# Pair products in another order, values split in place, evictions ahead of splits: a two-layer hybrid encoder block on one core

## The chip, the cores and the metric

The kernel runs on one NeuronCore of a Trainium2 chip. The metric is the time of one execution on the device in microseconds (us); the median of several runs is compared.

## The reference

Two layers on 512 frames of width 1024, in float32. Each layer normalises x, multiplies it with one wide matrix and feeds two recurrent branches, then a feed-forward part and a gated embedding:

```python
h = rmsnorm(x, norm1_g[i]);  z = h @ w_in[i] + b_in[i]
# branch A: mLSTM, 4 heads, dk = dv = 256 (q, k through a causal convolution and swish)
y_m = sigmoid(mo) * head_layernorm(mlstm(mq, mk, mv, mi, mf), m_norm_g[i])
# branch B: retention, 4 heads, dk = 256, dv = 512, rotary on q and k, decay per head
y_r = silu(rg) * head_layernorm(retention(rope(rq), rope(rk), rv), r_norm_g[i])
x = x + (sigmoid(gm) * (y_m @ w_bm[i]) + sigmoid(gr) * (y_r @ w_br[i])) @ w_out[i]
h2 = rmsnorm(x, norm2_g[i])
x = x + square(relu(h2 @ w_ff1[i] + b_ff1[i])) @ w_ff2[i] + b_ff2[i]
h3 = rmsnorm(x, norm3_g[i])
x = x + sigmoid(h3 @ w_pe_gate[i]) * (p[i] @ w_pe[i])
# after both layers: rmsnorm(x, final_g)
```

## The kernel before, in words

**Matmuls.** Every operand is split into a high part, rounded to the PE's format, and a low part, the rest; a product is three matmuls: high x high, high x low, low x high. All weights stream from HBM as *units*, in the order of `unit_list`. A `T8` unit is 128 output columns of a 1024-row matrix (24 matmuls of 512 columns). A `V` unit serves values, `PE` the embedding. A `PAIR` unit is 256 output columns in a scheme with seven products instead of eight (P1 to P7, each 12 matmuls of 256 columns): queries and keys of the retention, some gates, and the second feed-forward matrix. A `WIDE` unit is the same for the retention's values.

**Pieces of a pair.** P1 and P5 use piece A, P6 and P2 piece B, P3 and P7 piece C, P4 piece D. A, B and C are loaded into *raw* buffers of 128x1024 float32 (`fill_raws`, on SP's queue, four buffers plus one more in the first part of a layer); `prep_next` splits them: ACT writes the high part `wh`, DVE the low part `wl` (line 287). DVE makes the second half of B from A and C (line 421) and D from both halves of B (line 424). Sums of weight blocks that the loads read (`t1`, `t3`, `t2`) are made in HBM by accumulating DMAs on POOL's queue (`step`, line 331), paced along the matmuls. Split pieces have three buffers, D has one. `in_order` keeps loads, and splits on ACT and on DVE, in the order of the program. The order before is A, C, B, D.

**Banks.** Within a pair the products share PSUM banks: P1, P6, P7, P4 accumulate in one (a), P5 and P3 in another (c), P2 has a third (b). After each product the sum so far is read out (`done`, the *eviction*): in `pair_tiles` by ACT or DVE, in `ff2` by DVE adds into x (lines 1398, 1400). So P6 waits for the eviction of P1, P3 for that of P5, P7 for that of P6, P4 for that of P7. `run_pair` issues P1, P5, then `flush()`, then P6, P2, P3, P7; P4 is put into `later` and run by the next `flush()`, which is in the next pair, after four k steps of a `T8` tile, in the first block of an attention, before a head's scores, or after the first transposed tile of the gating.

**Order of instructions.** The program is written with a framework that gives each instruction a priority by its place in the program. A planner then fixes the order on each engine ahead of the run: with estimated durations, each engine takes the ready instruction that stands earliest in the program. On the chip every engine runs its list in that order.

**Retention.** For heads 0 and 2 a `WIDE` unit makes the values of two heads; those of the second are written to HBM (`rv_spill`) and read back by `rv_load` on POOL's queue into four of the six temporary tiles, then split into the value tiles. `r_gates` makes two gate tiles of a head by a pair, `r_out` the other two, transposes the four normalised output tiles (`back`) and multiplies and splits each.

**Norms.** A norm has one tile for its sum of squares and one for the factor of each frame, shared by all norms. The feed-forward part runs in four blocks `b`, each a group of `T8` pairs (`ff1`) and four `PAIR` units (`ff2`, o00 to o33); the embedding's two units stand before the last four pairs, and `flush()` after them.

Names in the trace: `l0r2o1a` is layer 0, retention, head 2, second gate pair, bank a; `l0r1brq`, `l0r1brk` are the query and key pairs of head 1; `l0o12` is the feed-forward pair of block 1, columns 2; `wh_A` is the high part of a piece A.

Of the kernel before, what the change touches and what calls it, by code (L numbers as in the profile page):

```python
# [42 lines left out]
P = 128  # L43
# [10 lines left out]
LOOK = 2  # L54
WARM = 11
# [36 lines left out]
PIECE = {"A": ("B11", "t1"), "C": ("B22", "t3"), "B": ("B21",), "D": ()}  # L92
# [22 lines left out]
READY = {"P1": 2, "P4": 2, "P5": 3, "P2": 4, "P6": 4, "P3": 4, "P7": 5}  # L115
# [35 lines left out]
def unit_list(i):  # L151
# [77 lines left out]
    u.append(("PE", 0))  # L229
    u.append(("PE", 1))  # L230
    pairs(ff_order()[1])
# [4 lines left out]
def build(ctx, tc, ins, out):  # L236
# [114 lines left out]
    loads = [(n, x) for n, x in order if x != "D" and x not in (("t4", 0), ("t4", 1))]  # L351
# [4 lines left out]
    cur["room"], cur["more"] = (), None  # L356
# [5 lines left out]
    def fill_raws(most=RAWS + 1):  # L362
        while at["load"] < len(loads) and len(raws) + len(kept) < most:
            n, x = loads[at["load"]]
            r = None
            if n in cur["room"] and cur["more"] not in raws:
                cur["more"] = n, x
                r = cur["low"].tile([P, UN], F32, name=f"wr{at['load']}", tag="wrx", bufs=1)
            elif len(raws) - (cur["more"] in raws) >= RAWS:
                break  # L370
            raws[n, x] = r = r or wpool.tile([P, UN], F32, name=f"wr{at['load']}", tag="wr", bufs=RAWS)
# [18 lines left out]
    def prep_next():  # L390
# [3 lines left out]

        w = Q if x == "D" else UN
# [8 lines left out]
        if r is None:  # L404
            r = raws.pop((n, x))
        if gates:
# [10 lines left out]
        if x == "A" or wide and x[0] == "t2":  # L417
            kept[n, x] = r
        elif x == "C":

            ve.tensor_tensor(raws[n, "B"][:, Q:], kept.pop((n, "A"))[:, Q:], r[:, :Q], OP.add)  # L421
        elif x == "B":

            ve.tensor_tensor(r[:, :Q], r[:, :Q], r[:, Q:], OP.add)  # L424
            formed[n, "D"] = r
        elif wide and x[0] == "B21":
            t = cur["br"].tile([P, UN], F32, name=f"t4{n}_{x[1]}", tag=("ph", "pl")[x[1]])
            ve.tensor_tensor(t, kept.pop((n, ("t2", x[1]))), r, OP.add)
            formed[n, ("t4", x[1])] = t

# [41 lines left out]
    def run_pair(name, act, done):  # L472
# [68 lines left out]
    def pair_tiles(name, act, consume, y=None):  # L541

        y = y or [tmp(f"{name}y{d}") for d in range(2)]
        a, b = slice(0, S), slice(S, T)

        def done(x, o):
            if x == "P1":
# [11 lines left out]
            else:  # L559
                ac.activation(y[0][:, a], o, AF.Copy)  # L560
                consume(y)

        run_pair(name, act, done)
# [38 lines left out]
    class Norm:  # L602


        def __init__(self, name, i, gain, act=None, j0=0, j1=NT):
# [20 lines left out]
        def square(self, k, x, add=None):  # L626
            w = self.n * P
            x = x[:, self.s]
            if self.sum is None:
                pl = cur["last"] if self.half else opool  # L630
                sq = pl.tile([P, w if self.half else T], F32, name=f"{self.name}sum", tag="ssum", bufs=1)[:, :w]
# [58 lines left out]
        def spread(self):  # L690
# [11 lines left out]
            pl = cur["last"] if self.half else opool  # L702
            self.b = pl.tile([P, w if self.half else T], F32, name=f"{n}rb", tag="rb", bufs=1)[:, :w]
# [51 lines left out]
    def scores(nm, qh, ql, kh, kl, decay):  # L755

        flush()
# [18 lines left out]
    def attend(nm, pt, vh, vl, c0, n, num):  # L776
        ph, pl, offs = pt
        for j in range(NT):
# [5 lines left out]
            if j == 0:  # L784
# [116 lines left out]
    cur["room"] = range(room)  # L901
# [17 lines left out]
    for i in range(L):  # L919
        act_side, ph_side = ("right", "left") if i == 0 else ("left", "right")  # L920
        xa = n1.act
        if i:
            cur["low"] = phase(f"low{i}", ph_side)
            cur["tmp"], cur["ntmp"] = cur["low"], NTMP
            cur["room"] = range(i * NU // L, i * NU // L + room)
# [165 lines left out]
        def r_gates(h, w, gs):  # L1091
# [6 lines left out]
            pair_tiles(f"l{i}r{h}o{w}", xs, consume)  # L1098

        def r_out(h, num, y, gs=None):  # L1100
# [91 lines left out]
        def rv_load(h):  # L1192

            v = value_tiles(f"l{i}r{h}")
            for j in range(NT):
                t = tmp(f"l{i}r{h}vr{j}")
                gp.dma_start(t, rv_dram[i, h // 2, j])
                split(t, v[0][j][:, :T], v[1][j][:, :T])
            return v

# [102 lines left out]
        vv = rv_load(3)  # L1303
        pt = r_scores(3, qk)
        yr = acts(cur["br"], f"l{i}yr1")
# [85 lines left out]
        def ff2(b, p):  # L1391
            started = set()

            def add(q, o, op):
                y = x[2 * p + q // 2][:, (q % 2) * S:(q % 2 + 1) * S]
                if b == 0 and q not in started:
                    started.add(q)
                    ve.scalar_tensor_tensor(y, y, bcol(i, "bf2", 2 * p + q // 2), o, OP.add, op)
                else:
                    ve.tensor_tensor(y, y, o, op)  # L1400

            def done(x_, o):
# [13 lines left out]
                if b == 3 and p and x_ in ("P6", "P7"):  # L1416
# [22 lines left out]
        n3 = Norm(f"l{i}n3", i, "g3", acts(n3_pool, f"l{i}n3"))  # L1439
# [3 lines left out]
        for u in range(2):  # L1443
            _, wh, wl = unit("PE")
            for c in range(4):
# [18 lines left out]
        nn = ([Norm(f"l{i}n4{a}", i, "gf", None, 2 * a, 2 * a + 2) for a in range(2)] if last  # L1464
# [205 lines left out]
```

## Time and profile before

| | |
|---|---|
| Runs | 2347.84, 2348.01, 2348.44 us; median 2348.01 |
| Profiled execution | 2347.49 us, span from first to last instruction 2345.8 us |
| PE busy | 2320.2 us (99%), 13660 matmuls |
| DVE, ACT, POOL busy | 1722.9 us (73%), 1218.9 us (52%), 245.7 us (10%) |
| Granted TensorE clock | 0.997 on the mean |
| HBM | 212 GB/s over the span |

Busy time counts a matmul from its start to its modelled end, and matmuls overlap; a wait of PE is read from the starts of its matmuls. L442 to L444 are the matmuls of a `T8` unit, L491 to L493 those of a pair, L534 to L536 those of a wide unit.

### The profile page before, as it was taken

The numbers are of one execution on the slowest core, as the hardware profiler recorded it, in microseconds if no ns is written. First come the engines' busy times: TensorE is split into PE (matmuls) and PEld (weight loads), VectorE is DVE, ScalarE is ACT, GpSimd is POOL, SyncE is SP. The second block draws the span as 40 slices with busy tenths as digits, with TensorE's granted clock in tenths as the row PEclk, the third lists the DMA queues.
The fourth block names the chain that finished last, engine by engine and source line by source line (L and its number), as shares of the span: only waits on it lengthen the run. The fifth ranks groups of instructions, "written<-read, shape, count | busy, mean of one in ns | idle before, by whom it ended". The sixth has DMA issues, their size and how long they took to land. (4 is left out here: it accounts for less than half of the span.)

```text
span 2345.8 us, 35261 instructions
## 1 busy us (share of the span) xinstructions
PE 2320.2 (99%) x13660; PEld 2056.2 (88%) x13660; DVE 1722.9 (73%) x2658; ACT 1218.9 (52%) x1768; POOL 245.7 (10%) x369
## 2 busy tenths in 40 slices
PE   9999999999999999999999999999999999999998
PEld 7888899898898898899888888998989988998997
DVE  7878767895675577677878787778958656776785
ACT  6656444553554445446557564454536445445454
POOL 3111101100102100000321110000000020000012
PEclk9999999999999999999999999999999999999999
DMA  5666676667578667676775645434343542433431
GB/s 201 187 180 172 218 229 170 205 189 202 168 230 269 195 198 189 199 219 181 206 221 169 182 124 186 136 126 158 108 158 104 166 153 96 130 108 98 132 117 59
DMA packets 146631, 394.89 MB, mean 168 GB/s; under 512 B 15376, under 2 KB 18832, under 8 KB 146464
## 3 DMA queue, kind: packets, MB, share of 16 engines
q1 hardware_dynamic: 99952, 247.77, 32.0%
q0 software_dynamic: 31104, 117.45, 20.4%
q10 hardware_dynamic: 15408, 27.43, 3.3%
q8 instruction: 107, 1.75, 0.3%
q14 instruction: 60, 0.49, 0.1%
HBM read 373.71 MB, written 123.73 MB: 212 GB/s over the span
## 5 line engine op out<-in xcount | busy, mean ns | idle before, releaser
L286 ACT ACTIVATE wh<-wr 128x1024 fp32r<-128x1024 f32 (+1 forms) x223 | 232.2, 1044 | 276.5 <-issue 69.6
L287 DVE TENSOR_TENSOR wl<-wr,wh 128x1024 fp32r<-128x1024 f32 (+1 forms) x221 | 271.9, 1232 | 77.7 <-ACT wh L286 77.5
L286 ACT ACTIVATE wh_B<-wr 128x1024 fp32r<-128x1024 f32 x100 | 105.9, 1059 | 159.2 <-PE l0f L443 8.5
L287 DVE TENSOR_TENSOR wl_B<-wr,wh_B 128x1024 fp32r<-128x1024 f32 x100 | 121.9, 1219 | 32.5 <-ACT wh_B L286 32.3
L286 ACT ACTIVATE wh_D<-wr 128x512 fp32r<-128x512 f32 x76 | 48.0, 632 | 124.9 <-DVE wr L424 65.4
L286 ACT ACTIVATE wh_C<-wr 128x1024 fp32r<-128x1024 f32 x76 | 80.2, 1056 | 61.3 <-issue 9.2
L286 ACT ACTIVATE wh_A<-wr 128x1024 fp32r<-128x1024 f32 x76 | 79.9, 1052 | 54.7 <-PE l1f L443 9.0
L287 DVE TENSOR_TENSOR wl_C<-wr,wh_C 128x1024 fp32r<-128x1024 f32 x76 | 94.3, 1240 | 18.7 <-ACT wh_C L286 18.5
L287 DVE TENSOR_TENSOR wl_A<-wr,wh_A 128x1024 fp32r<-128x1024 f32 x76 | 92.7, 1220 | 17.3 <-ACT wh_A L286 17.3
L442 PE MATMUL l1f<-l1n2h,wh 128*128 128x512 f32 x256 | 99.8, 390 | 0.0
L442 PE MATMUL l0f<-l0n2h,wh 128*128 128x512 f32 x256 | 99.8, 390 | 0.0
L444 PE MATMUL l0f<-l0n2h,wl 128*128 128x512 f32 x256 | 99.7, 389 | 0.0
L444 PE MATMUL l1f<-l1n2h,wl 128*128 128x512 f32 x256 | 99.7, 389 | 0.0
L443 PE MATMUL l1f<-l1n2l,wh 128*128 128x512 f32 x256 | 99.6, 389 | 0.0
L443 PE MATMUL l0f<-l0n2l,wh 128*128 128x512 f32 x256 | 99.6, 389 | 0.0
L287 DVE TENSOR_TENSOR wl_D<-wr,wh_D 128x512 fp32r<-128x512 f32 x76 | 52.4, 689 | 33.2 <-ACT wh_D L286 31.7
L421 DVE TENSOR_TENSOR wr<-wr,wr 128x512 f32<-128x512 f32 x76 | 52.1, 686 | 14.6 <-DMA wr<-wpairs 13.1
L444 PEld LDWEIGHTS l0f<-l0n2h,wl 128*128 128x128 f32 x256 | 48.0, 188 | 10.2
L444 PEld LDWEIGHTS l1f<-l1n2h,wl 128*128 128x128 f32 x256 | 48.1, 188 | 10.1
L443 PEld LDWEIGHTS l1f<-l1n2l,wh 128*128 128x128 f32 x256 | 48.1, 188 | 9.8
L442 PEld LDWEIGHTS l0f<-l0n2h,wh 128*128 128x128 f32 x256 | 48.1, 188 | 9.8
L442 PEld LDWEIGHTS l1f<-l1n2h,wh 128*128 128x128 f32 x256 | 48.1, 188 | 9.7
(5625 smaller groups left out, 8357.9 us busy)
## 6 DMA issues: line engine op xcount, KB each, us to landing
wr<-wstream SPq DMA_DIRECT2D x219, 512.0 KB, 4.2
wr<-wpairs SPq DMA_DIRECT2D x228, 256.0 KB, 2.8
wr<-wwide SPq DMA_DIRECT2D x24, 512.0 KB, 4.0
s0t<-wwide POOLq DMA_DIRECT2D x5, 1024.0 KB, 7.8
s4t<-wwide POOLq DMA_DIRECT2D x5, 1024.0 KB, 9.0
s12t<-wwide POOLq DMA_DIRECT2D x5, 1024.0 KB, 8.1
s16t<-wwide POOLq DMA_DIRECT2D x5, 1024.0 KB, 8.5
s1t<-wpairs POOLq DMA_DIRECT2D x4, 1024.0 KB, 6.7
```

The source lines that it names most:

```text
L286: a = ac.activation(hi_ap, src, AF.Copy)
L287: return a, ve.tensor_sub(lo_ap, src, hi_ap.bitcast(F32))
L421: ve.tensor_tensor(raws[n, "B"][:, Q:], kept.pop((n, "A"))[:, Q:], r[:, :Q], OP.add)
L442: te.matmul(o, sh, mh, start=first, stop=False)
L443: te.matmul(o, sh, ml, start=False, stop=False)
L444: cur["mm"] = te.matmul(o, sl, mh, start=False, stop=last)
```

## The change

- The products of a pair run as P1, P5, P2, P6, then `flush()`, then P3, P7; with `early` the flush stays after P5. Splits go A, B, C, D; loads still A, C, B, and the half of B that needs A and C is made just before B's split. P3 asks for one piece more ahead.
- Evictions of a pair, in `pair_tiles` and `ff2`, are given the priority of 250 instructions earlier.
- `rv_load` is parted: `rv_fetch` reads the values straight into the low value tile, right after the attention of the head before; `rv_split` splits them in place after the scores.
- `scores` has no `flush()`; the attention of heads 1 to 3 flushes after its second block.
- In `r_out`, two gate tiles are transposed and multiplied after P3 of the second gate pair, the other two are transposed after the pair and multiplied with the next `flush()`, behind P4.
- The norm's two tiles become one of 128x1024, handed from norm to norm, and between the first `WIDE` unit and `w_out` it serves as one more raw buffer.
- The second embedding unit moves behind the last four pairs, with a `flush()` after its third tile.

```diff
+AHEAD = 250
-PIECE = {"A": ("B11", "t1"), "C": ("B22", "t3"), "B": ("B21",), "D": ()}
+PIECE = {"A": ("B11", "t1"), "B": ("B21",), "C": ("B22", "t3"), "D": ()}
-READY = {"P1": 2, "P4": 2, "P5": 3, "P2": 4, "P6": 4, "P3": 4, "P7": 5}
+READY = {"P1": 2, "P4": 2, "P5": 3, "P2": 4, "P6": 4, "P3": 5, "P7": 5}
...
     u.append(("PE", 0))
+    pairs(ff_order()[1])
     u.append(("PE", 1))
-    pairs(ff_order()[1])
...
+    swap = {"B": "C", "C": "B"}
+    loads = [(n, swap.get(x, x)) for n, x in order if x != "D" and x not in (("t4", 0), ("t4", 1))]
+    wide0 = unit_list(0).index(("WIDE", (0, "rv0"), 0))
+    where = {n + i * NU // L: ("low", "one") if n >= wide0 else ("low",) for i in range(L) for n in range(room)}
+    free, taken = ["low", "one"] + list(range(RAWS)), {}
+    def norm_tile():
+        return opool.tile([P, 2 * T], F32, name="nr", tag="nr", bufs=1)
+    def raw_tile(a):
+        if a == "one":
+            return norm_tile()
+        pl, tag = (cur["low"], "wrx") if a == "low" else (wpool, f"wr{a}")
+        return pl.tile([P, UN], F32, name=f"wr{at['load']}", tag=tag, bufs=1)
...
+            fits = where.get(n, ()) if n * L // NU == cur["layer"] else ()
+            a = next((a for a in free if a in range(RAWS) or a in fits), None)
+            if a is None:
                 break
+            free.remove(a)
+            taken[n, x] = a
+            raws[n, x] = r = raw_tile(a)
...
+        if x == "B":
+            ve.tensor_tensor(r[:, Q:], kept.pop((n, "A"))[:, Q:], raws[n, "C"][:, :Q], OP.add)
+            give((n, "A"))
...
-        elif x == "C":
-            ve.tensor_tensor(raws[n, "B"][:, Q:], kept.pop((n, "A"))[:, Q:], r[:, :Q], OP.add)
+        elif x == "D":
+            give((n, "B"))
...
-    def run_pair(name, act, done):
+    def run_pair(name, act, done, early=False, mid=None):
...
-        product("P1")
-        product("P5")
-        flush()
-        for x in ("P6", "P2", "P3", "P7"):
+        for x in ("P1", "P5", "P2", "P6", "P3", "P7"):
             product(x)
+            if x == ("P5" if early else "P6"):
+                flush()
+            if x == "P3" and mid:
+                mid()
         later.append(last)
...
+    def ahead():
+        return tc.high_priority(AHEAD)
...
         def done(x, o):
+            with ahead():
+                evict(x, o)
+            if x == "P4":
+                consume(y)
...
     def scores(nm, qh, ql, kh, kl, decay):
-        flush()
...
-            if j == 0:
+            if j == turn:
                 flush()
...
-            attend(nm, pt, vv[0], vv[1], 0, 512, num)
+            attend(nm, pt, vv[0], vv[1], 0, 512, num, int(h > 0))
...
-            r_gates(h, 1, gs)
-            for v in range(4):
-                o = back(nm, num, v)
-                if v == 0:
-                    flush()
+            def gate(v, o):
                 ve.scalar_tensor_tensor(gs[v], o, bcol(i, "grn", 4 * h + v), gs[v], OP.mult, OP.mult)
                 split(gs[v], y[0][(4 * h) % 8 + v], y[1][(4 * h) % 8 + v])
+            def turn(a):
+                return [(v, back(nm, num, v)) for v in (a, a + 1)]
+            r_gates(h, 1, gs, mid=lambda: [gate(*t) for t in turn(0)])
+            o = turn(2)
+            later.insert(0, lambda: [gate(*t) for t in o])
...
-        def rv_load(h):
+        def rv_fetch(h):
             v = value_tiles(f"l{i}r{h}")
             for j in range(NT):
-                t = tmp(f"l{i}r{h}vr{j}")
-                gp.dma_start(t, rv_dram[i, h // 2, j])
-                split(t, v[0][j][:, :T], v[1][j][:, :T])
+                gp.dma_start(v[1][j][:, :T].bitcast(F32), rv_dram[i, h // 2, j])
             return v
+        def rv_split(v):
+            for hi, lo in zip(*v):
+                split(lo[:, :T].bitcast(F32), hi[:, :T], lo[:, :T])
...
         num = r_attend(0, pt, vv)
+        vv = rv_fetch(1)
         gs = {}
         r_gates(0, 0, gs)
-        vv = rv_load(1)
         pt = r_scores(1, qk)
+        rv_split(vv)
...
-        r_gates(1, 0, gs)
+        r_gates(1, 0, gs, early=True)
...
         num = r_attend(2, pt, vv)
+        vv = rv_fetch(3)
         qk = r_qk(3)
...
-        vv = rv_load(3)
         pt = r_scores(3, qk)
+        rv_split(vv)
...
+                with ahead():
+                    if b == 0 and q not in started:
+                        started.add(q)
+                        ve.scalar_tensor_tensor(y, y, bcol(i, "bf2", 2 * p + q // 2), o, OP.add, op)
+                    else:
+                        ve.tensor_tensor(y, y, o, op)
...
-                if b == 3 and p and x_ in ("P6", "P7"):
+                if b == 3 and p and x_ in ("P3", "P7"):
                     tile3(2 * p - 2 + (x_ == "P7"))
...
+                if c == 2:
+                    flush()
+        embed(0)
         for _, b, p in rest:
             ff2(b, p)
-        flush()
+        embed(1)
```

More of the change, by code (lines that the diff above doesn't have):

```diff
@@ L355, in build, with fill_raws @@
     room = unit_list(0).index(("T8", "w_out", 0, 0))
-    cur["room"], cur["more"] = (), None
+    wide0 = unit_list(0).index(("WIDE", (0, "rv0"), 0))
[8 more added lines that the diff above has]
+        return pl.tile([P, UN], F32, name=f"wr{at['load']}", tag=tag, bufs=1)
     def halves(n):
         return [slice(0, Q), slice(Q, UN)] if n == 1 else [slice(0, UN)]
-    def fill_raws(most=RAWS + 1):
-        while at["load"] < len(loads) and len(raws) + len(kept) < most:
+    def fill_raws(most=None):
+        while at["load"] < len(loads) and at["load"] != most:
             n, x = loads[at["load"]]
[L365 to L369, printed above, removed]
+            fits = where.get(n, ()) if n * L // NU == cur["layer"] else ()
+            a = next((a for a in free if a in range(RAWS) or a in fits), None)
+            if a is None:
                 break
-            raws[n, x] = r = r or wpool.tile([P, UN], F32, name=f"wr{at['load']}", tag="wr", bufs=RAWS)
+            free.remove(a)
+            taken[n, x] = a
+            raws[n, x] = r = raw_tile(a)
             if x:
@@ L629, in square @@
             if self.sum is None:
-                pl = cur["last"] if self.half else opool
-                sq = pl.tile([P, w if self.half else T], F32, name=f"{self.name}sum", tag="ssum", bufs=1)[:, :w]
+                if self.half:
+                    sq = cur["last"].tile([P, w], F32, name=f"{self.name}sum", tag="ssum", bufs=1)
+                else:
+                    self.own = self.own or norm_tile()
+                    sq = self.own[:, 0:w]
             else:
@@ L701, in spread @@
             te.matmul(o[:, :w], ones_r, dl, start=False, stop=True)
-            pl = cur["last"] if self.half else opool
-            self.b = pl.tile([P, w if self.half else T], F32, name=f"{n}rb", tag="rb", bufs=1)[:, :w]
+            self.b = self.own[:, T:T + w]
             ac.activation(self.b, o[:, :w], AF.Copy)
@@ L900, in build @@
     cur["tmp"], cur["ntmp"] = cur["low"], NTMP
-    cur["room"] = range(room)
+    cur["layer"] = 0
     n1 = Norm("l0n1", 0, "g1", acts(xa_pool, "l0n1"))
@@ L924, in build @@
             cur["tmp"], cur["ntmp"] = cur["low"], NTMP
-            cur["room"] = range(i * NU // L, i * NU // L + room)
+            cur["layer"] = i
         cur["br"] = phase(f"br{i}", ph_side)
```

37 lines of the change are left out of this document (19 added, 18 removed).

## The prediction

> **What bounds the kernel now.** I read the page first, for the shares of the engines.
>
> ```profile
> span 2345.8 us, 35261 instructions
> PE 2320.2 (99%) x13660; PEld 2056.2 (88%) x13660; DVE 1722.9 (73%) x2658; ACT 1218.9 (52%) x1768; POOL 245.7 (10%) x369
> ```
>
> TensorE (PE) is never idle for long: 2345.8 - 2320.2 = 25.6 us in all. The change adds and removes no matmul, so it can only move waits of PE. The waits of PE by releaser, longest first, show which ones there are (total, times, longest):
>
> ```profile
> PE l0r2o1a L491 <- ACT wh_A L286: 3.4, 1, 3.4
> PE l1o33a L491 <- DVE l1x L1400: 1.6, 1, 1.6
> PE l0o33a L491 <- DVE l0x L1400: 1.3, 1, 1.3
> PE l0m0vp L747 <- DVE wl L287: 1.3, 1, 1.3
> PE l0r0o0a L491 <- DVE l0r0o0y L558: 1.2, 1, 1.2
> PE l1r0o0a L491 <- DVE l1r0o0y L558: 1.2, 1, 1.2
> PE warm L905 <- POOL ones_r L275: 1.1, 1, 1.1
> PE l0r1brqa L491 <- DVE l0r1brqy L558: 1.0, 1, 1.0
> ...
> PE l0o12a L491 <- DVE l0x L1400: 0.7, 1, 0.7
> ```
>
> Seven of these rows are on line 491, in the pair units, 10.4 us together. The rest of the idle time (start, mLSTM part, end) lies where the diff does nothing.
>
> Idle time understates a wait here. The timeline of PE, and the granted clock by stretches, say by how much (start, duration; then stretch, PE, PEld, DVE, ACT, POOL, PEclk, DMA):
>
> ```profile
> 608.73 0.41 PE L491 MATMUL l0r2o0c<-l0xsh,wh_C 128*128 128x256 f32 x1
> 608.94 0.41 PE L492 MATMUL l0r2o0c<-l0xsl,wh_C 128*128 128x256 f32 x1
> 609.44 0.28 PE L492 MATMUL l0r2o0c<-l0xsl,wh_C 128*128 128x256 f32 x1
> 609.56 0.28 PE L493 MATMUL l0r2o0c<-l0xsh,wl_C 128*128 128x256 f32 x1
> 603.70:609.30 5.60, 5.16 (x22) 4.87 (x23) 4.06 (x10) 2.79 (x8) 0.00 (x0) 0.51 0.35 115
> ```
>
> At full clock a matmul of a pair starts 0.12 us after the one before but counts as busy for 0.28, so 0.28 - 0.12 = 0.16 us of each wait is not seen as idle. After the one wait of 3.4 us the granted clock is 0.51 for 5.6 us, and matmuls start every 0.21 us: 0.09 us lost on each of the 24 that ran there, 2.2 us more. [...]
>
> **The change part by part.** *Values in place, fetched early (worth 5.8 us).* Why did ACT hold the weight piece back by 3.4 us? ACT's timeline, the tiles' landing times (layer 0, then layer 1) and POOL's timeline:
>
> ```profile
> 598.58 0.63 ACT L286 ACTIVATE l0r3vh<-l0r3vr 128x512 fp32r<-128x512 f32 x1 [2.83 <-DMA l0r3vr<-rv_spill]
> 602.69 1.04 ACT L286 ACTIVATE wh_A<-wr 128x1024 fp32r<-128x1024 f32 x1
> DMA to landing us min/median/max: 4.4/11.1/12.1
> DMA to landing us min/median/max: 2.8/3.0/3.0
> 587.23 0.90 POOL L331 DMA_DIRECT2D s8t<-wpairs  x1 [9.98 <-DMA br_spill<-l0brs]
> 587.88 1.95 POOL L1197 DMA_DIRECT2D l0r3vr<-rv_spill  x3
> ```
>
> The reload of head 3's values is issued at 587.88, right behind a step of the weight sums, and lands after 11.1 us (3.0 in layer 1, where none is ahead). ACT takes its instructions in order, so wh_A stands behind that split. The new `rv_fetch(3)` stands before `r_qk(3)` and the eight `w_br` tiles, with all of their matmuls between it and its split, and needs none of the six temporary tiles. On POOL it waits for PE's last read of the value tile; behind it are only the next weight sums. Wait 3.4 + 0.16 + 2.2 of half clock = 5.8 us gone. At head 1 it is earlier by a pair and removes no wait.
>
> *Embedding unit behind the last pairs (3.2 us).* The two o33a rows are the last product P4 of the last feed-forward pair, waiting for the add that empties P7. Now three embedding tiles, 18 matmuls of 512 columns, stand between P7 and P4: with twice the columns of a pair's matmul some 0.24 us each, an estimate, over 4 us. 1.6 + 1.3 + 2 x 0.16 = 3.2 us. The two normalised tiles that follow P4 keep one embedding tile and six k steps of the gate product as cover; without it they would cost PE up to the 1.6 us of now.
>
> *No flush before the scores; flush after P6 (2.6 us of 3.9).* In r0o0a and r1brqa PE waits in P4 for P7's add. Two products or a few score matmuls lie between now, four products afterwards. r1brqa gives 1.0 + 0.16 = 1.2. For the two r0o0a rows, 2 x (1.2 + 0.16) = 2.7, DVE has little room:
>
> ```profile
> 403.00:430.00 27.00, 25.78 (x209) 25.30 (x208) 24.78 (x46) 19.61 (x32) 4.70 (x7) 1.00 0.62 203
> ```
>
> DVE is busy 24.78 of 27.00 us there, so some of the wait may come back at the next piece of weights. I take half, 1.4. The gating in two turns does the same instructions, with two transposed tiles more held in PSUM; I cost it at nothing, because the next head's attention or a pair covers it. If that cover fails it is a wait like r0o0a's, 1.4 us a layer.
>
> *Eviction priority, B before C, raw buffers (0.9 + 4.7 us).* o12a, an eviction behind a split, gives 0.7 + 0.16 = 0.9. Besides, going through the starts of PE's matmuls, I count 71 places in the pairs that are late by less than 0.3 us. The first and the last:
>
> ```profile
> 330.04 0.28 PE L493 MATMUL l0bgm2c<-l0xsh,wl_A 128*128 128x256 f32 x1
> 330.32 0.39 PE L491 MATMUL l0bgm2a<-l0xsh,wh_B 128*128 128x256 f32 x1
> 2285.34 0.39 PE L491 MATMUL l1o33a<-l1hh,wh_D 128*128 128x256 f32 x1 [1.58 <-DVE l1x L1400]
> 2285.56 0.28 PE L492 MATMUL l1o33a<-l1hl,wh_D 128*128 128x256 f32 x1
> ```
>
> They are late by 0.28 - 0.12 = 0.16 and 0.22 - 0.12 = 0.10; at 0.10 each, 7.1 us. Many are pieces B, which were prepared third and used second, or followers of a large wait. I take two thirds, 4.7 us; bounds 0 and 7.1.
>
> *What it costs.* The planner keeps the pieces in order, and there is one buffer for D, so D of a pair is split only after P4 of the pair before, and the next A only after D. In a feed-forward pair of now:
>
> ```profile
> 1023.41 0.28 PE L491 MATMUL l0o22a<-l0hh,wh_A 128*128 128x256 f32 x1
> 1023.65 0.28 PE L493 MATMUL l0o22a<-l0hh,wl_A 128*128 128x256 f32 x1
> 1026.24 0.28 PE L491 MATMUL l0o21a<-l0hh,wh_D 128*128 128x256 f32 x1
> 1027.65 0.28 PE L491 MATMUL l0o22a<-l0hh,wh_B 128*128 128x256 f32 x1
> 1027.83 0.63 ACT L286 ACTIVATE wh_D<-wr 128x512 fp32r<-128x512 f32 x1 [2.31 <-PE l0o21a L493]
> 1028.36 1.05 ACT L286 ACTIVATE wh_A<-wr 128x1024 fp32r<-128x1024 f32 x1
> 1028.56 0.41 DVE L1400 TENSOR_TENSOR l0x<-l0x,l0o21a 128x256 f32<-128x256 f32 x1
> 1029.83 1.21 DVE L287 TENSOR_TENSOR wl_A<-wr,wh_A 128x1024 fp32r<-128x1024 f32 x1
> ```
>
> A product takes 1027.65 - 1026.24 = 1.41 us. From the end of P4 (1027.65) until A is whole (1029.83 + 1.21 = 1031.04) it takes 3.39 us. Now four products follow P4; afterwards two, P3 and P7, and A's low part is first read by the third matmul, 1023.65 - 1023.41 = 0.24 later: 2 x 1.41 + 0.24 = 3.06 us. It is short by 0.33. The planner can put the first two matmuls of P5 ahead, which leaves 0.33 - 0.24 = 0.09. Such transitions: pairs whose predecessor's P4 is still behind, 12 in the feed-forward part and 5 in the retention part of a layer, 34 in all. 34 x 0.09 = 3.1 us; bounds 0 and 34 x 0.33 = 11.2. Second, where no P4 is behind (16 pairs a layer), only P3 lies between P6 and P7, which need the same bank: 1.41 us for 0.28 of the matmul, the 0.41 of the add and at worst a split of 1.21 in its way, 1.90. P1 and P6 stand so now, and the waits show hardly any; I take one such loss, 0.5 us, bounds 0 and 4 (eight). The shared norm tile and the extra raw buffer I cost at nothing: loads start earlier, and where the tile serves as a buffer its norm has been used up.
>
> **Sum.** 5.8 + 3.2 + 2.6 + 0.9 + 4.7 = 17.2 gained, 3.1 + 0.5 = 3.6 paid: 13.6 us off the profiled execution's 2347.49 us (span 2345.8 and 1.7 around it). The median of the runs is 2348.0, so 2334.4. All gained and nothing paid is 20.9, 2327; half gained and 4 paid is 2348.0 - 8.6 + 4 = 2343.4.
>
> **The rivals.** *A: weights become the wait (slower).* If the chain from P4 to A stretches, every one of the 34 transitions stalls. It decides at 17.2 / 34 = 0.51 us each. The row at 1028.56 shows how: with priority one more add of 0.41 can go ahead of wl_A, 0.33 + 0.41 = 0.74, and 34 x 0.74 = 25 us: 2356. Against it: the chain above already holds one add, and evictions are split between ACT and DVE in the retention part. Chance 0.08.
>
> *B: loads land too late.* B is now loaded last, behind C, into the buffer of the last C.
>
> ```profile
> 1013.82 0.88 POOL L331 DMA_DIRECT2D s16t<-wwide  x1 [8.14 <-PE l0o20a L493]
> 1015.54 0.33 SPq L379 DMA_DIRECT2D wr<-wpairs  x1
> 1024.46 1.06 ACT L286 ACTIVATE wh_B<-wr 128x1024 fp32r<-128x1024 f32 x1 [2.68 <-DMA wr<-wpairs]
> ```
>
> Beside a weight sum (1013.82) a load took 1024.46 - 1015.54 = 8.9 us until its split began. The next B can be loaded when C's split is over (1.05 + 1.21, some 2.4 us into a pair), so its split would begin at 11.3. P2 of the next pair comes at 9 x 1.41 = 12.7, and two splits must be over by then: 12.7 - 1.05 - 1.21 = 10.4. That is 0.9 us late; in each of the 12 pairs of layer 0's feed-forward part that follow a pair it makes 10.8 us, and 2348.0 - 17.2 + 3.6 + 10.8 is 2345. [...] Against B: sums run beside only some loads, and the retention part gets a buffer more. Chance 0.08.
>
> *C: the change does less than it says.* The order on every engine is fixed ahead by a planner from estimates, and priority only chooses among what it thinks ready. If the evictions stay where they are, only the early fetch and the embedding unit count: 5.8 + 3.2 - 3.6 = 5.4, 2342.6. Chance 0.10.
>
> **How the numbers follow.** Forecast 2334.4 with chance 0.74, its own range 2327 to 2343.4 from the two ends of the sum, and one us below for waits elsewhere that earlier loads may shorten. With B and C 2326 to 2346, which leaves out A and edges. About 0.2% (4.7 us) is what a measurement can tell from no change. Faster by more: the forecast, most of C and a little of B, 0.83. Within: the rest of both, 0.09. Slower: A, 0.08.
>
> **What would show it.** Right: no l0r2o1a wait on ACT, clock 1.0 throughout the retention part, no o33a and r0o0a rows, PE's idle time near 16 us. Wrong: rows of PE waiting for wl_A or wh_A at nearly every second pair of a block (A), for wh_B behind DMA in layer 0 (B), or the same r0o0a and r1brqa rows again (C).

## The result, and the profile after

Forecast: 2334.4 us. Measured: 2359.11 us median (2358.42 to 2359.59), against 2347.93 for the kernel before: ratio 1.0045, 95% interval 1.0031 to 1.0059. The change makes the kernel slower by 11.2 us. The profiled execution took 2358.42 us, its span is 2356.7, 10.9 above the span of before. The first rows of the page:

```profile
span 2356.7 us, 35318 instructions
PE 2327.9 (99%) x13660; PEld 2057.3 (87%) x13660; DVE 1719.4 (73%) x2658; ACT 1212.0 (51%) x1768; POOL 250.4 (11%) x369
```

The matmuls are as many as before, and idle time is 2356.7 - 2327.9 = 28.8 us instead of 25.6; the prediction's sign of being right was 16. The waits of PE by releaser (total, times, longest) show that the rows named in the prediction are gone, and what came for them:

```profile
PE l1r2s L463 <- ACT l1r2kh L287: 1.7, 1, 1.7
PE l0r2s L463 <- ACT l0r2kh L287: 1.7, 1, 1.7
PE l1r3brqa L512 <- ACT l1r3brqy L580: 1.6, 1, 1.6
...
PE l0r3brqa L512 <- ACT l0r3brqy L580: 0.8, 1, 0.8
PE l0r0o1a L514 <- DVE wl_A L288: 0.8, 1, 0.8
PE l1r0o1a L514 <- DVE wl_A L288: 0.8, 1, 0.8
PE l0o33c L514 <- DVE wl_C L288: 0.8, 1, 0.8
PE l0o12b L514 <- DVE wl_B L288: 0.8, 1, 0.8
PE l0o22b L514 <- DVE wl_B L288: 0.8, 1, 0.8
```

Rows of idle time understate (1.75 us before the first matmul of l0r2s, which starts 1.91 us late), so I compare starts: the *lateness* of a group of matmuls is the sum, over its starts, of the distance to the start before less that of full clock (0.118 us for a pair's 256 columns, 0.227 for 512, the commonest distances in the traces of both kernels). It can be below zero, because in some stretches matmuls of 256 columns start every 0.114 us. Summed over all groups it rose by 10.95 us, which is the change of the span. By groups, layer 0 and layer 1:

| group | before | after | change |
|---|---|---|---|
| r2o0 + r2o1 (wait for wh_A) | 7.10, 1.52 | 0.31, 0.31 | -6.8, -1.2 |
| r0o0 and r1brq (wait for P7's add) | 2.87, 1.59 | 0.94, 1.63 | -1.9, 0 |
| o33 | 1.66, 1.72 | 1.19, 0.54 | -0.5, -1.2 |
| r3brq | 0.07, 0.06 | 2.50, 3.24 | +2.4, +3.2 |
| r2s, r1o0, r1o1 | 0.53, 0.53 | 5.08, 3.60 | +4.6, +3.1 |
| r0o1 | 0.06, 0.06 | 1.28, 1.26 | +1.2, +1.2 |
| all feed-forward pairs (o33 among them) | 3.75, 1.80 | 6.61, 2.08 | +2.9, +0.3 |

Besides layer 0's feed-forward pairs and r0o1, two places are new, and they are the largest. The first is the query pair of head 3. ACT's timeline there, and POOL's:

```profile
531.41 1.86 POOL L1233 DMA_DIRECT2D l0r3vl<-rv_spill  x3 [12.81 <-DVE l0r1o1y L1140]
533.51 0.56 POOL L1233 DMA_DIRECT2D l0r3vl<-rv_spill  x1 [0.24 <-PE l0r2a L465]
535.98 0.63 ACT L287 ACTIVATE l0r3vh<-l0r3vl 128x512 fp32r<-128x512 f32 x1 [2.02 <-DMA l0r3vl<-rv_spill]
537.49 0.63 ACT L287 ACTIVATE l0r3vh<-l0r3vl 128x512 fp32r<-128x512 f32 x1 [0.88 <-DMA l0r3vl<-rv_spill]
538.03 0.37 ACT L580 ACTIVATE l0r3brqy<-l0r3brqa 128x256 f32<-128x256 f32 x1
538.96 0.63 ACT L287 ACTIVATE l0r3vh<-l0r3vl 128x512 fp32r<-128x512 f32 x1 [0.56 <-DMA l0r3vl<-rv_spill]
```

The fetch is early as promised, and so are the splits: nothing in the program holds them back but the load, and the planner has put them directly behind the fetch, far ahead of the scores behind which `rv_split` stands. ACT takes its list in order, waits 2.02 us for the load, and the query pair's evictions (line 580) wait behind it. The wait has moved from one pair to another.

The second is head 2's scores, waiting for the key. ACT's timeline, the eviction of the query's P4 and the key's split, and PE's wait:

```profile
492.20 0.37 ACT L592 ACTIVATE l0r2brqy<-l0r2brqa 128x256 f32<-128x256 f32 x1
508.26 0.61 ACT L287 ACTIVATE l0r2kh<-l0r2brku 128x512 fp32r<-128x512 f32 x1
508.93 0.50 PE L463 MATMUL l0r2s<-l0r2qh,l0r2kh 128*128 128x512 f32 x1 [1.75 <-ACT l0r2kh L287]
```

### The profile page after: what moved, and what is told of

Read it like the earlier page. It is cut to its first block, busy times and chain, and to the rows that moved or that the text cites. A ratio compares the mean times of both kernels' runs of the same rounds, so it can differ in the third digit from the quotient of the medians.

```text
span 2356.7 us, 35318 instructions
## 1 busy us (share of the span) xinstructions
PE 2327.9 (99%) x13660; PEld 2057.3 (87%) x13660; DVE 1719.4 (73%) x2658; ACT 1212.0 (51%) x1768; POOL 250.4 (11%) x369
## 3 DMA queue, kind: packets, MB, share of 16 engines
q8 instruction: 107, 1.75, 0.3%
## 4 chain that ended last, share of the span: by engine, by line
PE 85%; issue 7%; DVE 4%; DMA 2%; ACT 1%; POOL 0%; DVEq 0%; ACTq 0%; POOLq 0%
PE l0f L463 2%; PE l1f L463 2%; PE l1f L465 2%; PE l1f L464 2%; PE l0f L464 2%; PE l0f L465 2%; PE l1br L465 1%; PE l0br L465 1%; PE l0br L463 1%; PE l1br L463 1%; PE l1br L464 1%; PE l0br L464 1%; DMA wr<-wpairs 1%; PE l0bm L463 1%; PE l0pg L463 1%
## 5 line engine op out<-in xcount | busy, mean ns | idle before, releaser
L287 ACT ACTIVATE wh<-wr 128x1024 fp32r<-128x1024 f32 (+1 forms) x213 | 220.9, 1043 | 258.7 <-issue 65.3
L288 DVE TENSOR_TENSOR wl<-wr,wh 128x1024 fp32r<-128x1024 f32 (+1 forms) x211 | 257.9, 1226 | 68.0 <-ACT wh L287 67.6
L287 ACT ACTIVATE wh_B<-wr 128x1024 fp32r<-128x1024 f32 x86 | 90.6, 1055 | 81.6 <-DMA wr<-wpairs 13.1
L288 DVE TENSOR_TENSOR wl_B<-wr,wh_B 128x1024 fp32r<-128x1024 f32 x86 | 105.0, 1221 | 26.5 <-ACT wh_B L287 26.0
L287 ACT ACTIVATE wh_D<-wr 128x512 fp32r<-128x512 f32 x66 | 41.4, 627 | 139.5 <-PE l0o01a L513 6.2
L287 ACT ACTIVATE wh_C<-wr 128x1024 fp32r<-128x1024 f32 x66 | 69.7, 1056 | 75.8 <-PE l1bm L464 12.2
L288 DVE TENSOR_TENSOR wl_C<-wr,wh_C 128x1024 fp32r<-128x1024 f32 x66 | 80.4, 1218 | 11.1 <-ACT wh_C L287 11.1
L288 DVE TENSOR_TENSOR wl_D<-wr,wh_D 128x512 fp32r<-128x512 f32 x66 | 45.4, 687 | 37.9 <-ACT wh_D L287 36.6
L464 PEld LDWEIGHTS l0f<-l0n2l,wh 128*128 128x128 f32 x256 | 48.1, 188 | 9.8
```

Source lines behind the costliest of these rows:

```text
L287: a = ac.activation(hi_ap, src, AF.Copy)
L288: return a, ve.tensor_sub(lo_ap, src, hi_ap.bitcast(F32))
L464: te.matmul(o, sh, ml, start=False, stop=False)
```

## The experiments

They ran on several chips, and on these the executions of one kernel lie further apart than in the first runs (the kernel before: 2344.6 to 2352.8). Medians are given with their ratio to the kernel before in the same session. What a place costs is read from the lateness of groups in the profiled execution, which is one execution: layer 0's feed-forward pairs move by 2 to 3 us between kernels that differ elsewhere, so a difference of that size there is not put down to an edit without rows that show it.

**1. Values split behind.** In the changed kernel:

```diff
+                a, _ = split(lo[:, :T].bitcast(F32), hi[:, :T], lo[:, :T])
+                if mm:
+                    tc.add_manual_dep(a.ins, mm.ins.name, SYNC, reason="values behind a matmul")
...
+            if c == 1:
+                mm = cur["mm"]
```

> The changed kernel, but head 3's values are split only after the second of the eight tiles behind the query and key pair (one added dependence, both layers); everything else stays. Theory W (the loss is three local waits): the four splits no longer stand in front of the evictions of the query pair on ACT while their load is in flight, so the rows of PE waiting for l0r3brqy and l1r3brqy on ACT (0.8 to 1.6 us each) go, and with them the 2.4 and 3.2 us that this pair starts later: 2359.1 - 5 = 2354, at least 3 us less. Theory O (the new order of products costs a little in every pair, and these waits only collect what is late anyway): the time comes back in the next pair, 2358 to 2359.5. No theory expects a wait for ACT before head 2's second gate pair.

Measured: 2351.15, ratio 1.0010 (1.0001 to 1.0019), span 2347.2. ACT's timeline at the same place:

```profile
532.00 0.60 ACT L816 ACTIVATE l0r2num<-l0r2a 128x512 f32<-128x512 f32 x1 [0.79 <-PE l0r2a L465]
533.43 0.39 ACT L580 ACTIVATE l0r3brqy<-l0r3brqa 128x256 f32<-128x256 f32 x1 [0.83 <-PE l0r3brqa L514]
```

The lateness of r3brq fell from 2.50 and 3.24 to 0.22 in both layers, 5.3 us, and did not come back in the next pair: theory W. The span fell by 9.5; the rest is 1.0 of half clock in l0r1o1, 0.4 and 0.6 in r0o0, and 2.3 in layer 0's feed-forward pairs, which the edit does not touch.

**2. The query's last product earlier.** `pair_tiles(..., early=a == 1)` for the key pair.

> The changed kernel, but in the key pair of every head the last product of the query pair runs after P5, as it did before, not after P6. Theory W: the query's P4 comes one product (1.4 us) and the place of P2 earlier, so rope of the query and then of the key is done earlier on DVE, and head 2's scores no longer wait for l0r2kh and l1r2kh (1.7 us each as rows): r2s 4.4, the add behind it in r1o0 2.0, and the half clock after it in layer 0, 1.1, make some 6 to 7 us; some 1 us may come back as a wait of the query's P4 for P7's add. 2352 to 2354. Theory O: the place of P4 matters little for the scores, DVE is simply full; within 1.5 us of 2359.1.

Measured: 2350.32, ratio 1.0007 (0.9997 to 1.0016), span 2346.4. The timeline shows the key pair's first matmul and the beginning of the query's rope on DVE, in the kernel before, in the changed kernel, then here:

```profile
484.34 0.29 PE L491 MATMUL l0r2brka<-l0xnh,wh_A 128*128 128x256 f32 x1
490.05 0.74 DVE L1064 SCALAR_TENSOR_TENSOR l0r2brqu<-l0r2brqy,bc,l0cos 128x512 f32<-128x512 f32 x1
```

```profile
484.38 0.29 PE L512 MATMUL l0r2brka<-l0xnh,wh_A 128*128 128x256 f32 x1
492.94 0.74 DVE L1097 SCALAR_TENSOR_TENSOR l0r2brqu<-l0r2brqy,bc,l0cos 128x512 f32<-128x512 f32 x1
```

```profile
483.67 0.28 PE L512 MATMUL l0r2brka<-l0xnh,wh_A 128*128 128x256 f32 x1
489.62 0.75 DVE L1097 SCALAR_TENSOR_TENSOR l0r2brqu<-l0r2brqy,bc,l0cos 128x512 f32<-128x512 f32 x1
504.81 0.50 PE L463 MATMUL l0r2s<-l0r2qh,l0r2kh 128*128 128x512 f32 x1 [0.54 <-ACT l0r2kh L287]
```

From the start of the key pair to rope it is 5.71 us before, 8.56 in the changed kernel and 5.95 here, and the wait for the key falls from 1.75 to 0.54. r2s, r1o0 and r1o1 together fell from 8.68 to 2.58 over both layers, 6.1 us: theory W again. The span fell by 10.3: 1.6 also went in r0o0, 1.7 in layer 0's feed-forward pairs, 1.4 in layer 1's r3brq and 1.0 in the gate pair bgm2, and some 1.5 us came back in other places.

**3. No priority**, and **4. pieces prepared as before.** In the changed kernel, one at a time:

```diff
-        return tc.high_priority(AHEAD)
+        return ExitStack()
```

> The changed kernel without the priority of evictions (they keep their own place in the program's order). Theory W: priority is not what cost; the time stays within 2 us of 2359.1, because the waits named sit at a DMA, at rope and at loads. Theory P (evictions ahead of splits make the low parts late: rows for wl_A, wl_B, wl_C on DVE, 8 rows of 0.3 to 0.8 in the changed kernel, 5 us together, plus half of the chain P4, D, A): 2353 or less, and the wl rows go.

Measured: 2370.55, ratio 1.0096 (1.0081 to 1.0111). Both theories were wrong: priority does not cost, it is worth 12.6 us here. Without it P1's eviction comes too late for P6, though P5 and P2 lie between: the starts of P6 (piece B into bank a) that are late by more than 0.03 us went from 3.9 to 16.7 us together, and PE's waits have rows such as

```profile
PE l1r1o0a L512 <- ACT l1r1o0y L580: 1.2, 1, 1.2
PE l0o12a L512 <- DVE l0x L1442: 1.0, 1, 1.0
```

> The changed kernel with the pieces prepared in the order of before (A, C, B, D), the half of B that needs A and C made at C's turn, the raw buffer of A and C given back there, and P3 asking for as many pieces ahead as before. Products keep the new order. Theory W: the waits for wh_B and wl_B beside weight sums in layer 0's feed-forward part go (o12, o13, o22: 0.8, 0.9 and 1.7 us by start-to-start, 3.4 together), and B, now split third and used second, is late by about 0.1 in the pairs; between 2355.5 and 2359. Theory O: the order of the pieces fits the order of the products, and taking the one back without the other costs: 2361 or more, with rows of PE waiting for wl_B or wh_B in both layers.

Measured: 2370.18, ratio 1.0094 (1.0079 to 1.0109). The waits for wh_B went, as theory W said, and two larger ones came. PE's waits, and DVE's timeline in front of the first:

```profile
PE l0o11a L511 <- DVE l0x L1441: 4.2, 1, 4.2
PE l0o21a L511 <- DVE l0x L1441: 3.0, 1, 3.0
```

```profile
941.69 0.69 DVE L435 TENSOR_TENSOR wr<-wr,wr 128x512 f32<-128x512 f32 x1 [7.11 <-DMA wr<-wpairs]
942.30 0.41 DVE L1441 TENSOR_TENSOR l0x<-l0x,l0o11b 128x256 f32<-128x256 f32 x1
```

The half of B that is made from A and C now needs B's load at C's turn; DVE waits for it with three evictions behind. It is the picture of r3brq on another engine, and the reason why the change's order of pieces belongs to its order of products.

Both places of the changed kernel went here too, though neither the values nor the flush were touched: r3brq fell to 0.22 us and r2s to 0.08 in both layers. ACT's timeline shows the splits of head 3's values in front of the same evictions:

```profile
532.83 0.64 ACT L287 ACTIVATE l0r3vh<-l0r3vl 128x512 fp32r<-128x512 f32 x1 [0.35 <-DMA l0r3vl<-rv_spill]
533.89 0.36 ACT L579 ACTIVATE l0r3brqy<-l0r3brqa 128x256 f32<-128x256 f32 x1
```

The reload lands after a median of 3.1 us here, 5.6 in the changed kernel (layer 1: 3.5 and 6.4), and ACT waits 0.35 instead of 2.02. The query's rope begins as late as in the changed kernel, 8.57 us behind the start of the key pair, but the key is ready in time; a part of the delay shows in r1o0 instead (0.7 more in each layer). So the two steps make the waits possible, and their size hangs on the order of the pieces too. Why the reload is slower in the changed kernel is open.

**5. Both edits of 1 and 2.**

> The changed kernel with both edits at once: head 3's values split behind the second of the eight tiles, and the query pair's last product after P5 of the key pair. Theory W (local waits): the two savings add, less the 1.4 us of layer 1's query pair of head 3 that both removed: the profiled span 2356.7 - 9.5 - 10.3 + 1.4 = 2338, some 8 us under the kernel before (ratio about 0.9965). Rival N (a part of either saving was loads landing at luckier times in layer 0's feed-forward part, where 2 us moved in both): 2342, within 0.2% of before (ratio 0.998 or more).

Measured: 2345.40, ratio 0.9986 (0.9978 to 0.9995), span 2340.1. The two savings nearly add in the span (16.6 of 18.4 us), but the profiled execution was the fastest of eleven. By the ratio, 0.998 or more, it is rival N.

**6. Priority alone, on the kernel before.**

> The kernel before with one part of the change: evictions of a pair get the priority of 250 instructions earlier. The change's own order of products lost 12.7 us of span when priority was taken from it. Theory S (priority is needed because P7 now follows P6 with only P3 between): in the old order two products lie between everywhere, so it gives at most the 0.9 us of the o12a row and a little of the small late places: 2346 to 2349. Rival G (evictions behind splits cost in any order): 2342 or less.

Measured: 2359.32, ratio 1.0047 (1.0033 to 1.0061). Neither: alone, priority costs 11 us, most of it in the feed-forward pairs (lateness 3.75 to 13.98 in layer 0, 1.80 to 4.46 in layer 1). DVE waits there for a load to make the half of B, and the eviction that PE waits for stands behind it. DVE's timeline, and PE's row:

```profile
1027.06 0.69 DVE L422 TENSOR_TENSOR wr<-wr,wr 128x512 f32<-128x512 f32 x1 [4.87 <-DMA wr<-wpairs]
```

```profile
PE l0o21a L492 <- DVE l0x L1407: 2.8, 1, 2.8
```

**7. Embedding unit back**, in the kernel of 5.

> The kernel with both edits, but with the second embedding unit back in front of the last four pairs and the flush directly behind them. By the prediction's step the move of the unit is worth 3.2 us: two waits of P4 for the add that empties P7 come back, as rows o33a of 1.3 and 1.6, and the span is 3.2 above the one with both edits. By the trace of the changed kernel the move was worth 1.65 (a wait for wl_C in o33c took part of its place): 1.5 to 2 above.

Measured: 2356.50, ratio 1.0029 (1.0017 to 1.0041), span 2354.7, 14.6 above number 5 (the median 11.1), far more than either expectation. The o33a rows for l0x did not come back. In their place, layer 1 as layer 0, stand

```profile
PE l0o33c L514 <- DVE wl_C L288: 1.4, 1, 1.4
PE l0pg L464 <- DVE l0n3l L656: 1.3, 2, 0.7
```

o33 is later by 2.6 us and the gate product that reads the normalised tiles (pg) by 6.8, over both layers; most of the rest is in o03, o12, o13 of layer 0. The unit's move is worth at least 9 us in this order, as cover for those tiles.

**8. P4' after P5 everywhere** (`early=True` as default), values split behind. P4' is the last product of the pair before.

> The changed kernel with values split behind, and the last product of a pair after P5 of the next one everywhere, not after P6 (so the order P1 P5 P4' P2 P6 P3 P7). The prediction charged 3.1 us to having only P3 and P7 between P4' and the next A; that should come back: -3 against the kernel with both edits. It credited 2.6 us to four products instead of two between P7 and P4'; that should be lost, as rows r1brqa and r0o0a of about 1. Theory R (room behind P7 counts): 0 to +3 against the kernel with both edits. Theory A (room before the next A counts): -1 to -4.

Measured: 2341.49, ratio 0.9968 (0.9957 to 0.9979), span 2339.6: the fastest so far, 7.4 us under the kernel before. Against number 5 the median is 3.9 us lower, the span 0.5. Lateness at the reads of A in bank a (starts late by more than 0.03 us) fell from 2.7 to 0.2 us, as theory A says; r0o0 became later by 0.3 and 0.1 only. But the starts of P4' rose from 0.5 to 4.6 us, 4.4 of it in three of layer 0's feed-forward pairs, whose lateness went from 2.4 to 4.7:

```profile
PE l0o11a L512 <- DVE l0x L1446: 1.7, 1, 1.7
PE l0o02a L512 <- DVE l0x L1446: 1.2, 1, 1.2
PE l0o21a L512 <- DVE l0x L1446: 0.8, 1, 0.8
```

There P4' waits for P7's add, so the room behind P7 counts as well, as theory R says, where weight sums run beside (number 14).

**9 to 11, on the kernel of 8: gating in one turn; no norm tile as raw buffer; P6 evicted by DVE.**

> The kernel of the last experiment (values split behind, last product after P5 of the next pair everywhere, profiled span 2339.6), but the gating of a head in one turn behind its second gate pair, as in the kernel before. The prediction costed the two turns at nothing: then the span stays within 1 us of 2339.6. Rival T (two turns spread DVE's and ACT's work of a head over a pair, and in one turn the next piece of weights comes late): 3 to 8 us more, with rows for wl or wh in the pair or the attention behind each of the four heads of a layer.

Measured: 2344.16, ratio 0.9983 (0.9974 to 0.9992), span 2341.9: r2o1 late by 1.2 more in each layer. The span rose by 2.3 us, between the two expectations: small, but not nothing.

> The same base (2339.6), but the norm tile no longer serves as a raw buffer. The prediction costed the buffer at nothing beyond loads that start earlier: 0 to +2. Rival L (in the retention part a load that starts a buffer later lands behind its split, as at two other places of these kernels): +3 or more, as rows behind DMA on ACT or DVE in the retention part of layer 0, where weight sums run, and hardly in layer 1.

Measured: 2348.05, ratio 0.9994 (0.9985 to 1.0004), span 2347.4, 7.8 more, all in layer 0, 5.0 of it in the three retention places below: rival L. Another 3.0 is in o21, a feed-forward pair beside which the buffer isn't used, and is not shown to be the buffer's.

```profile
PE l0r1brqa L512 <- DVE l0r1brqy L590: 1.9, 1, 1.9
PE l0r2o0a L512 <- DVE l0r2o0y L590: 1.3, 1, 1.3
PE l0gr2a L512 <- DVE l0gr2y L590: 1.1, 1, 1.1
```

In front of the first, DVE is idle for 4.90 us until it makes the half of B, at 386.49 instead of 378.19. The profile names no releaser for it; that a load stands behind it is argued from SP, which issues the loads there 3 to 4 us later than in number 8.

> The same base (2339.6), but in pair_tiles P6 is read out by DVE instead of ACT. In the changed kernel P7's first matmul is 0.10 late and its second again 0.10 in nearly every pair without a pending P4, because ACT has begun a split of 1.06 us about 0.15 before P6 ends. Theory E (a split in front of the eviction on ACT): on DVE the eviction finds a free engine more often, the 0.20 goes in most of the 20 such pairs of the retention parts: -2 to -4. Rival F (DVE's own splits of 1.21 stand in front as often, and DVE is the fuller engine): 0 to +4.

Measured: 2345.86, ratio 0.9991 (0.9982 to 1.0001), span 2344.0. Both: 0.2 us each went in fifteen pairs (brq, brk, bgm3, r2o0, r3o0), as E said, and as F said DVE was late elsewhere (r2brq 2.5 in layer 0, r0o1, r3brq), so that the span rose by 4.4. ACT's and PE's timelines in the changed kernel show what E means:

```profile
314.64 1.06 ACT L287 ACTIVATE wh_B<-wr 128x1024 fp32r<-128x1024 f32 x1 [1.53 <-issue]
315.60 0.36 ACT L586 ACTIVATE l0r0brqy<-l0r0brqa 128x256 f32<-128x256 f32 x1
315.80 0.28 PE L514 MATMUL l0r0brqc<-l0xsh,wl_C 128*128 128x256 f32 x1
316.02 0.39 PE L512 MATMUL l0r0brqa<-l0xsh,wh_C 128*128 128x256 f32 x1
316.25 0.28 PE L513 MATMUL l0r0brqa<-l0xsl,wh_C 128*128 128x256 f32 x1
```

The split of 1.06 us, begun at 314.64, just before P6's last matmul (started at 314.39, 0.28 long) ended, holds the eviction of P6 until 315.60 in spite of its priority. P7 starts 0.22 after P3's last matmul and its second matmul 0.23 later, 0.10 lost twice.

**12. The values alone, on the kernel before.**

> The kernel before with one part of the change, the values: read straight into the low value tile right after the attention of the head before, split in place (head 3's behind the second of the eight tiles), no temporary tiles. The prediction's step: the wait of 3.4 us with its half clock goes, 5.8 us; by start-to-start the group of l0r2o0 and l0r2o1 lost 6.8 in layer 0 and 1.2 in layer 1, so 2345.8 - 6 to 8 = 2338 to 2340 of span. Rival: weights take over as the wait in the same pairs, 2343 or more.

Measured: 2342.39, ratio 0.9972 (0.9961 to 0.9984), span 2342.3, between the two expectations. The lateness of r2o0 and r2o1 fell by 7.3 us; r0o0, r0o1 and head 1's scores around head 1's splits became later by 3.1. This one part of the change is faster than the kernel before by 6.1 us, and isn't told apart from number 8.

**13 to 15. Without the weight sums** of layer 1: in the changed kernel, in that of 8, in the kernel before.

> The changed kernel without the weight sums of layer 1, which run beside layer 0's feed-forward part; layer 1 loads blocks given in HBM in their place, as many bytes, so its numbers are not the reference's and only its time is meant. Theory B (the sums slow the loads of B): the lateness of layer 0's feed-forward pairs falls from 6.6 to layer 1's 2.1, the span from 2356.7 to about 2352, and the rows of PE waiting for wh_B and wl_B of l0o12, l0o13 and l0o22 go. Otherwise (the order on the engines): 6 or more stays, 2356.

> The repaired kernel (values split behind, last product after P5 everywhere, span 2339.6), without the weight sums of layer 1 as in the run before. Theory B: the lateness of layer 0's feed-forward pairs falls from 4.7 to layer 1's 0.3, the span to 2335, and the rows of PE waiting for l0x in o02, o11, o21 go (1.2, 1.7, 0.8: DVE stands for a load there in front of the eviction). Otherwise 4 or more stays.

> The kernel before without the weight sums of layer 1. Control: its layer 0 feed-forward pairs are 2.2 late in all, layer 1's 0.0, most of the 2.2 in o33 (1.7, in both layers) and o12 (0.9). Theory B: o12 goes, 0.9, and the span falls by about 1 from 2345.8; a fall of 4 or more would say that the sums cost the kernel before as much as the changed one, and the change is not what made loads late.

Measured: spans 2351.1, 2333.0, 2341.9; medians 2352.96, 2335.45 (of two runs), 2344.97; ratios 1.0025 (1.0016 to 1.0035), 0.9946 (0.9929 to 0.9964), 0.9987 (0.9977 to 0.9997). Lateness of the feed-forward pairs, layer 0 and layer 1: 1.7 and 2.4 (was 6.6 and 2.1); -0.9 and -0.9 (was 4.7 and 0.3); 0.6 and 0.3 (was 3.75 and 1.80). The 2.2 and 0.0 of the last expectation leave out o33's P4, 1.5 and 1.8 us late behind the first matmuls of the gate product. In all three layer 0's excess over layer 1 goes: it is the sums. In the kernel before the excess is 1.9 us, in the changed one 4.5.

By the whole span the sums cost 5.6 us in the changed kernel, 6.6 in that of 8, and 3.9 in the kernel before, where the expectation had set 4 as the line at which the change is not what made loads late. So most of their cost was there before, and the change added some 1.7 us by the spans, 2.6 by the excess of layer 0. The rows of o12, o13 and o22 for wh_B and wl_B, and in number 14 those of number 8 for l0x, are gone; in the changed kernel ACT had stood there like this:

```profile
1027.67 1.06 ACT L287 ACTIVATE wh_B<-wr 128x1024 fp32r<-128x1024 f32 x1 [3.47 <-DMA wr<-wpairs]
```

**16. Head 1's values behind a matmul too**, on the kernel of 8.

> The repaired kernel (2339.6), with head 1's values too split only after a matmul behind their load (the last one of head 1's scores). Theory: the same cause as at head 3, smaller: the pairs r0o0 and r0o1 are late by 1.4 in layer 0 and 0.8 in layer 1, and 1 to 1.5 of it goes. Rival: the splits then fall into the second gate pair, where ACT and DVE also gate the head, and r0o1 becomes later by as much.

Measured: 2340.09, ratio 0.9969 (0.9957 to 0.9981), span 2342.0. r0o0 and r0o1 fell by 1.4 us in all, as the theory said; layer 0's feed-forward pairs, which the edit does not touch, were 3.2 later in the profiled execution. Not told apart from number 8; both beat both kernels.

## Why the prediction was wrong, point by point

Two steps turned the sign: the splits of the values were taken to run where the program has them (5.6 us lost), and P4 was taken to free only a bank (7.6 us lost). With both mended, number 5, the sign is that of the forecast.

- *Values, 5.8 us.* The wait went, and more: 6.8 in layer 0 and 1.2 in layer 1. The step that failed is "with all of their matmuls between it and its split". That is the program's order. The planner takes what it thinks ready, as the prediction itself says under rival C, and it put these splits in front of the matmuls; tied behind one of them they cost nothing (number 1). ACT's wait of 2.02 us suggests that the load took longer than planned for; the planner's estimate itself was not read. Price 5.6 in the changed kernel; where the reload landed sooner the same order cost hardly anything (number 4). That the fetch at head 1 "removes no wait" left out a cost: the places around head 1's splits became later by 3.1 on the kernel before (number 12), and tying them back gave 1.4 (number 16).
- *Flush after P6, 2.6 us.* At the places it names it held in part: r1brq -1.1 in layer 0, r0o0 -1.0 over both. The step that failed is that it was costed for P7's add alone. P4 carries more than a bank: in the key pair it completes the query, and rope, the key and the scores follow from it on DVE, which is busy for 15.65 us of the 16.00 from 492.3 to 508.3 in the changed kernel (number 2). Price 7.6 in r2s, r1o0 and r1o1, of which 6.1 went with the old place of the flush in the key pair alone. r0o1 rose by 2.3, where I had allowed half of r0o0's wait to come back; whether that is the next piece's wait or head 1's splits (numbers 12 and 16) is not told apart.
- *Embedding unit, 3.2 us.* The o33a rows went; a wait for wl_C took part of the place, so 1.65 net. Its worth in this order was mis-sized: "cost PE up to the 1.6 us of now" was 6.8 at the gate product (number 7).
- *71 small late places, 4.7 gained.* Counted in one way (starts of pairs late by 0.03 to 0.3 us) there were 89 before with 9.7 us and 151 after with 14.4. The gain came: P6, P3 and P4 fell from 7.8 to 2.9 us. What failed is "one such loss, 0.5 us, bounds 0 and 4": P6 had stood one product behind P1, the new order puts P7 in that place behind P6, and the starts of P7 went from 0.2 to 4.9 us. P2, put at nothing, rose from 0 to 1.8.
- *Chain from P4 to A, 3.1 us.* Right in size: among the same small places the starts of A in bank a rose from 1.5 to 4.8 us, and 2.5 came back when a third product stood there (number 8).
- *Priority 0.9, gating and buffer nothing.* Single prices don't exist here: priority loses 11 on the old order and saves 12.6 on the new; in the order of number 8 the two turns are worth 2.3 and the buffer some 5.0, at its three places.
- *Rivals.* A's time, 2356, was nearest, but not by its mechanism: rows for wl_A at every second pair are not there. B is shown in kind, at some 2 us more than before instead of 10.8 (numbers 13 and 15). What I lacked was a rival in which a moved wait lands on another engine's list.

With the two failed steps mended alone the change is 3.5 us faster than the kernel before (0.9986, number 5); with the flush after P5 everywhere it is 7.4 us (0.9968, number 8), where 13.6 were forecast. The values alone give 6.1 (number 12), so the rest of the change together is not shown to be worth anything.

## What to carry to other kernels

In these traces an instruction that waited for a load held up the evictions behind it on its engine (after a wait of 2.02 us on ACT in the changed kernel, of 7.11 on DVE in number 4), so before moving a load ask where the planner will put its consumer, and tie the consumer to work that ends after the load. When a product is moved, follow what its result completes, not only the bank that it frees. Parts of a reordering have no prices of their own: measure them taken out of the new order as well as put into the old.

## What the runs showed of the hardware

Behind the same wait before head 2's scores the granted clock fell in one place and not in another. The stretches behind it (stretch, PE, PEld, DVE, ACT, POOL, PEclk, DMA share, GB/s) in layer 0 and layer 1 of the changed kernel:

```profile
508.90:514.10 5.20, 5.17 (x26) 4.99 (x27) 5.20 (x8) 3.11 (x4) 0.00 (x0) 0.67 0.32 106
1678.10:1683.30 5.20, 5.18 (x36) 4.97 (x37) 5.20 (x8) 3.10 (x4) 0.00 (x0) 1.00 0.33 104
```

Both layers wait alike, 1.91 us by the starts. In layer 0 the clock is 0.50 from 510.9 to 513.3, where matmuls of 256 columns start every 0.21 us. PE's rows have the wait at 1.7 us in both layers of the changed kernel, of number 1 and of number 13. In number 1 neither layer was slowed after it (l0r1o1 is 1.0 us less late than in the changed kernel), in number 13 layer 1 was (r1o1 late by 1.07 instead of 0.23) and layer 0 was not (layer 0, then layer 1 of number 13):

```profile
509.00:513.00 4.00, 3.71 (x26) 3.56 (x27) 4.00 (x7) 2.65 (x4) 0.00 (x0) 1.00 0.48 135
1672.00:1676.00 4.00, 4.00 (x22) 3.90 (x21) 4.00 (x6) 2.03 (x3) 0.00 (x0) 0.57 0.29 109
```

So behind this wait the half clock came in layer 0 of the changed kernel and in layer 1 of number 13, and not in the other layer; the pair behind it was later by 1.0 us (number 1) and 0.8 (1.07 less 0.23). What decides whether it comes, no run here shows.
